# Feed steps, weights by tokens, kept sums and norm weights on GpSimd in a one-layer hybrid decoder step

## The chip, the core and the metric

The kernel runs on one core of one Trainium2 chip. The metric is the time of one execution in device microseconds (us); smaller is better. Before the change three runs gave a median of 1971.52 us (1970.41 to 1973.65).

## The reference, cut to what matters

One layer of a decoder serves a prompt of 1024 tokens and a sample group of 8 sequences with 4 tokens each (1056 tokens in all), with the same weights, in float32:

```
mod = silu(c) @ w_ada + b_ada            -> shift1, scale1, gate1, shift2, scale2, gate2 per sequence
h   = LN(x) * (1 + scale1) + shift1
z   = h @ w_in + b_in                    (1024 -> 6664 columns)
merged = sigmoid(gm) * (mLSTM(z) @ w_branch_m) + sigmoid(ga) * (window_attention(z) @ w_branch_a)
x   = LN(alpha * x + gate1 * (merged @ w_out), ln1_g, ln1_b)
h2  = LN(x) * (1 + scale2) + shift2
u   = h2 @ w_up + b_up                   (1024 -> 5632 columns, a half and b half)
u'  = causal depthwise convolution of width 3 over tokens
f   = (gelu(u'_a) * u'_b) @ w_down + b_down      (2816 -> 1024)
x   = LN(alpha * x + gate2 * f, ln2_g, ln2_b)
```

The outputs are x for both groups, the mLSTM state, the attention caches and the last rows of u for the convolution.

## The kernel before

Activations lie transposed, features on the partitions and the 1056 tokens along the free axis, in 43 equal slots of SBUF ([128, 1056] each). `slot` takes the slot that has been free longest and `drop` returns one; whoever writes a slot anew waits for its last readers. Tokens are cut into three ranges TT of 384, 384 and 288; for the norms into nine row tiles (eight of 128 tokens, and tile 8 with the 32 sample tokens). Each product of two float32 operands is three matmuls of rounded parts (high x high, high x low, low x high); a weight is loaded as `wraw` by SP, rounded on ScalarE to `whi` (L429), and the rest `wlo` is taken on VectorE, in the down projection on GpSimd (L433). `Stream.prep(i)` writes these two, loading first if needed; `load(i)` issues DMAs up to weight i; `ahead_of(i)` preps i+1 and loads i+2. All DMAs spoken of here are issued by SP's queue, in order.

The order of instructions on every engine is the order in which the Python program writes them. TensorE's products are the main line. Work beside it is written as generators in `sides`: after each part of a product, `pulse` adds the part's length to a clock and lets the first generator go on by `rate` steps per us of that clock. What stands between two `yield`s is one step.

From 1060 us on the trace goes through these stages:

- Output projection (w_out) in three token ranges with three PSUM banks L in turn, evacuated by ScalarE (`scaled`, L1695, L1698). After each range a side `out_side` is appended: `residual` (transposes back to rows, VectorE's alpha-sum L1628 and statistics, `norm_factor` on GpSimd, `norm_act` on ScalarE L1604, gain on GpSimd L1635, bias on VectorE L1640, statistics and norm again, rows stored as x1D), then `make_h2` (transposes, ScalarE L1664 and L1669, VectorE L1670). Seven steps of `residual` and seven of `make_h2` per range.
- Up projection: five blocks by token ranges, three direct, sixteen pairs of blocks in a fast scheme (L1507), four direct again (L1752 evacuates on ScalarE). Blocks go to DRAM (uD, yD).
- Feed: a side that reads u back chunk by chunk (22 of 128 features), runs the convolution (`conv`: ScalarE's first tap L1762 with small copies L1763 to L1767, VectorE's two long taps L1769 and L1771, the sample taps L1773, L1774), gelu on ScalarE (L1866), the multiplication by the other half on VectorE (L1876), and the split into high (ScalarE L1884) and low (VectorE L1887). Gelu, multiplication and split belong to the chunk before the one whose taps run.
- Down projection in five groups of 5, 5, 4, 4, 4 chunks. The first three go column block by column block, `down_block` adds to eight tiles facc on VectorE (L1984). The fourth, `down_by_tokens`, goes token range by token range, two column blocks for each of its four weights (k counts 0 to 11), scales by gate2 on ScalarE (L2016), and when a range is done a side `pre` transposes its sums to rows (L198 into PD), adds alpha*x to them (L1945, x fetched from x1D at L1934) and stores the row tile as preD (L1947).
- Last stage: the fifth group, `product` (L2146), has tokens on the partitions: 24 matmuls of 512 columns for each row tile. `fetch` loads preD (L2128); VectorE multiplies by gate2 and adds (L2154, L2155) and takes statistics (L307 to L309); GpSimd makes the factor (L300, L301, L1600); ScalarE normalizes (L1604); the multiplication by ln2_g (L2172) is on GpSimd for the tiles in BY_POOL and on VectorE for the others; the addition of ln2_b (L2173) is on GpSimd; SP stores (L2180). Tile 8 runs on VectorE (L2177, L2178).

Of the kernel before, what the change touches and what calls it, by code (L numbers as in the profile page):

```python
# [11 lines left out]
F32 = mybir.dt.float32  # L12
# [3 lines left out]
OP = mybir.AluOpType  # L16
AX = mybir.AxisListType

D = 1024
# [13 lines left out]

RATE_T, RATE_U, RATE_V, RATE_D, RATE_P = 0.5, 0.5, 0.9, 0.8, 0.8
ROOM = 5
RATES = [0.442, 0.395, 0.35, 0.45, 0.463, 0.495, 1.0, 0.7, 0.417]


STRIPS = [(0, 256), (256, 256), (512, 256), (768, 128), (896, 128)]
# [66 lines left out]
def hybrid_step(ctx: ExitStack, tc: tile.TileContext, I, O):  # L106
# [18 lines left out]
    def slot(dt=F32, name="s"):  # L125
        i = free_slots.popleft()
        count[0] += 1
        t = slots.tile([128, TOK], dt, name=f"{name}_{count[0]}", tag=f"slot{i}", bufs=1)
        tag_of[id(t)] = (i, t, name)
        return t  # L130

    def drop(*ts):
        for t in ts:
            free_slots.append(tag_of.pop(id(t))[0])
# [379 lines left out]
    up_at, dn_at = [], []  # L514
# [852 lines left out]
    hf = {}  # L1367
# [226 lines left out]
    def rows_of(i):  # L1594
        return 128 if i < 8 else 32
# [10 lines left out]
    def residual(ti, r1, tiles, fetch, gb, bb_, done):  # L1606


        ids = [3 * ti + a for a in range(3)]
        st = {}  # L1610
        xs_ = {}
        fetch_at = {0: [0, 1], 1: [2]}
        for s in range(6):
            for a in fetch_at.get(s, ()):
                xs_[a] = fetch(ids[a])
            if s == 0:
                yield
            if s < 3:
                a, n = s, rows_of(ids[s])
                x = xs_[a]  # L1620
                for j in range(8):
                    src, off = r1[j]
                    transpose(pd(j)[:n], src[:, off + a * 128:off + a * 128 + n])
                if a == 2:
                    drop(*tiles)
                for hf in range(2):
                    c = slice(hf * 512, hf * 512 + 512)
                    V.scalar_tensor_tensor(x[:n, c], x[:n, c], ALPHA, PD[hf][:n], op0=OP.mult, op1=OP.add)  # L1628
                mv = ln_stats(x, n)
                st[a] = norm_factor(mv, n)  # L1630
            a = s - 1
            if 0 <= a < 3:
                n = rows_of(ids[a])
                norm_act(xs_[a], st[a], n)
                G.tensor_tensor(xs_[a][:n, :D], xs_[a][:n, :D], gb[:n, :D], op=OP.mult)  # L1635
            a = s - 2
            if 0 <= a < 3:
                n = rows_of(ids[a])
                x = xs_[a]
                V.tensor_tensor(x[:n, :D], x[:n, :D], bb_[:n, :D], op=OP.add)  # L1640
                done(ids[a], n, x)
                mv = ln_stats(x, n)
                st[a] = norm_factor(mv, n)
            a = s - 3
            if 0 <= a < 3:
                norm_act(xs_[a], st[a], rows_of(ids[a]))
            yield
        return [xs_[a] for a in range(3)]

    h2 = mrg  # L1650
# [154 lines left out]

    facc = []
    rows2 = {}
    preD = [dram.tile([128, D], F32, name=f"preD{i}") for i in range(9)]
    acts2 = []

    def kept_rows():
# [23 lines left out]
    def feed():  # L1835

        js, got = [j for c in chunks_of for j in c], {}

        def load(n):
            if n < len(js) and n not in got:  # L1840
                ds = [uD[js[n]], yD[22 + js[n]] if 22 + js[n] in yD else uD[22 + js[n]]]
                got[n] = [slot(name="ld") for _ in ds]
                for t, d in zip(got[n], ds):
                    S.dma_start(t, d)

        load(0)
        load(1)
        yield
        prev = None
        for n in range(len(js) + 1):  # L1850
            cur = None
            if n < len(js):
                while len(free_slots) < ROOM:
                    yield
                load(n + 1)
                j, (u, y2) = js[n], got.pop(n)
                if 22 + j not in yD:
                    u2, y2 = y2, slot(name="y")
                    yield from conv(22 + j, u2, y2)
                    drop(u2)  # L1860
                    yield
                cur = slot(name="y"), y2
                taps = conv(j, u, cur[0])
                next(taps)
            if prev:
                A.activation(prev[0], prev[0], AF.Gelu_apprx_tanh)  # L1866
            yield
            if cur:
                next(taps)
                if len(free_slots) > ROOM:  # L1870
                    load(n + 2)
            yield
            if cur:
                next(taps)
            if prev:
                V.tensor_tensor(prev[0], prev[0], prev[1], op=OP.mult)  # L1876
                drop(prev[1])
            yield
            if cur:
                next(taps, None)  # L1880
                drop(u)
            if prev:
                hi, lo = slot(F32R, "ahi"), slot(F32R, "alo")
                A.copy(hi, prev[0])  # L1884
            yield
            if prev:
                V.tensor_tensor(lo, prev[0], hi.bitcast(F32), op=OP.subtract)  # L1887
                drop(prev[0])
                acts2.append((hi, lo))
            yield  # L1890
            prev = cur
            if n == 10:
                yield from gate_rows2()
        yield from kept_rows()
# [28 lines left out]

    there = set()

    def pre(ti):

        xs_ = {}
        ids = [3 * ti + a for a in range(3)]

        def fetch(i):
            if i in ids:
                xs_[i] = slot(name="x1r")
                S.dma_start(xs_[i][:rows_of(i), :D], x1D[i][:rows_of(i)])  # L1934

        fetch(ids[0])
        for i in ids:
            n, x = rows_of(i), xs_[i]
            fetch(i + 1)
            for j in range(8):  # L1940
                transpose(pd(j)[:n], facc[j][:, i * 128:i * 128 + n])
            yield
            for hf_ in range(2):
                c = slice(hf_ * 512, hf_ * 512 + 512)
                V.scalar_tensor_tensor(x[:n, c], x[:n, c], ALPHA, PD[hf_][:n], op0=OP.mult, op1=OP.add)  # L1945
            yield
            S.dma_start(preD[i][:n], x[:n, :D])  # L1947
            there.add(i)
            drop(xs_.pop(i))
        if ti == 2:  # L1950
            drop(*facc)

# [8 lines left out]
    def operands(gi):  # L1961
        base = sum(KG[:gi])
        n = 0
        while len(acts2) < base + KG[gi]:
            step_side()
            n += 1
            assert n < 200
        return {k: acts2[base + k] for k in range(KG[gi])}
# [30 lines left out]
    def down_by_tokens(gi):  # L1999

        a = operands(gi)
        for ti in range(3):
            t0, nt = TT[ti]
            np_ = nt if ti < 2 else 256
            for q in range(4):
                s_ = dn_at[gi] + q
                k = ti * 4 + q
                if k < 3:
                    win.ahead_of(s_)
                elif k > 6 and k < 11:  # L2010
                    win.prep(dn_at[gi] + k - 3)
                    win.load(dn_at[gi] + k - 2)
                for j in (2 * q, 2 * q + 1):
                    down_block(gi, j, ti, a)
                    f = facc[j][:, t0:t0 + np_]
                    A.activation(f, f, AF.Copy, scale=modT[:, 5, j, 0:1])  # L2016
                    if ti == 2:
                        f = to3(facc[j][:, SEQ:])
                        V.tensor_tensor(f, f, mod_bcast(5, j), op=OP.mult)
                if ti == 2:  # L2020
                    win.done(s_)
            summed.append(ti)
            if not ti:
                spread(pre_rows(), 1.3)
        for k in a:
            drop(*a[k])
# [90 lines left out]
    rate[0] = RATES[6]  # L2117
    gi = len(KG) - 1
    a = operands(gi)
    ln2g, ln2b = bcast_row(I["ln2_g"]), bcast_row(I["ln2_b"])  # L2120
    xs_ = {}

    def fetch(i):
        if i < 9:
            while i not in there:
                pulse(0.4)
            xs_[i] = slot(name="pre")
            S.dma_start(xs_[i][:rows_of(i), :D], preD[i][:rows_of(i)])  # L2128

    for i in range(3):  # L2130
        fetch(i)
    gp, gs = rows2["gp"], rows2["gs"]
    banks = deque([PG, PE_, PF, *L])
    bank_of = {}
    BY_POOL = (0, 2, 4)

    def product(i, hf):
        n, t0 = rows_of(i), i * 128
# [42 lines left out]
        drop(xs_.pop(i))  # L2181

    for i, hf in [(0, 0), (1, 0), (0, 1), (1, 1)] + [(i, hf) for i in range(2, 9) for hf in range(2)]:
        if hf == 0:
            fetch(i + 3)
        product(i, hf)
        add(i, hf)
        if hf:
            stats(i)
            if i:  # L2190
                gains(i - 1)
# [36 lines left out]
```

## Time and profile before

| | |
|---|---|
| median of three runs | 1971.52 us |
| the profiled execution | 1973.88 us, its span 1972.1 us |
| TensorE busy | 1909.6 us of the span, 97% |
| VectorE, ScalarE, GpSimd busy | 1077.3, 803.2, 470.6 us |
| mean granted TensorE clock | 0.991 of full speed |
| moved by DMA | 237.74 MB, 121 GB/s on average |

The span runs from the first to the last instruction. A share of busy time is a mean over stages with different limits; a busy PE is a modelled figure, since matmuls overlap. Idle time of an engine other than the limiting one costs nothing by itself.

### The profile page before, as it was taken

How to read it: one execution, taken by the hardware profiler on the slowest of the kernel's cores; microseconds unless marked ns; L12 is line 12 of the kernel's file. 1: busy time of each engine (PE TensorE's matmuls, PEld its weight loads, DVE VectorE, ACT ScalarE, POOL GpSimd, SP SyncE). 2: the span in 40 equal slices, each digit the busy share in tenths (PEclk: the TensorE clock that was granted, in tenths of full speed). 3: DMA queues.
4: the chain of work that ended last, by engine and by line, in shares of the span. 5: the costliest groups of instructions: out<-in, count | busy, mean ns of one | idle time of the engine just before them, and what ended most of it. 6: DMA issues, size and time to landing. Idle time of an engine off the chain costs nothing. (4 is left out here: it accounts for less than half of the span.)

```text
span 1972.1 us, 33018 instructions
## 1 busy us (share of the span) xinstructions
PE 1909.6 (97%) x12981; PEld 1818.6 (92%) x12981; DVE 1077.3 (55%) x2297; ACT 803.2 (41%) x1796; POOL 470.6 (24%) x591
## 2 busy tenths in 40 slices
PE   6999999999999999999999999999999998999887
PEld 4899999999999989898999999999999998999875
DVE  5454454444644445341454456766666567598658
ACT  4534334343555455331322355333333246654421
POOL 2013233232123031200000333134343310222127
PEclk9999999999999999999999999999999999999989
DMA  9151414334220312398424141432323365344363
GB/s 291 47 140 25 141 30 125 76 79 97 74 77 23 112 54 79 110 342 256 159 83 132 55 128 46 153 109 88 130 88 101 118 225 173 110 139 153 105 227 126
DMA packets 235302, 237.74 MB, mean 121 GB/s; under 512 B 11857, under 2 KB 207105, under 8 KB 235113
## 3 DMA queue, kind: packets, MB, share of 16 engines
q1 hardware_dynamic: 234365, 235.01, 38.9%
q8 instruction: 102, 1.67, 0.4%
q10 hardware_dynamic: 780, 0.61, 0.1%
q14 instruction: 55, 0.45, 0.1%
HBM read 174.93 MB, written 62.68 MB: 120 GB/s over the span
## 5 line engine op out<-in xcount | busy, mean ns | idle before, releaser
L455 PE MATMUL L<-hhi,whi 128*128 128x384 f32 (+1 forms) x1600 | 526.3, 329 | 0.1
L455 PE MATMUL L<-hlo,whi 128*128 128x384 f32 (+1 forms) x1600 | 517.2, 323 | 0.0
L455 PE MATMUL L<-hhi,wlo 128*128 128x384 f32 (+1 forms) x1600 | 516.7, 323 | 0.0
L455 PEld LDWEIGHTS L<-hhi,whi 128*128 128x128 f32 x1600 | 301.7, 189 | 6.6 <-issue 4.8
L455 PEld LDWEIGHTS L<-hlo,whi 128*128 128x128 f32 x1600 | 301.9, 189 | 0.3
L455 PEld LDWEIGHTS L<-hhi,wlo 128*128 128x128 f32 x1600 | 301.6, 188 | 0.0
L433 DVE TENSOR_TENSOR wlo<-wraw,whi 128x1024 fp32r<-128x1024 f32 (+1 forms) x89 | 108.5, 1220 | 114.4 <-ACT whi L429 112.9
L455 PE MATMUL L<-mhi,whi 128*128 128x384 f32 (+1 forms) x480 | 159.4, 332 | 7.8 <-ACT u L1752 3.6
L455 PE MATMUL L<-mhi,wlo 128*128 128x384 f32 (+1 forms) x480 | 156.5, 326 | 0.6 <-DVE wlo L433 0.6
L455 PE MATMUL L<-mlo,whi 128*128 128x384 f32 (+1 forms) x480 | 156.1, 325 | 0.0
L455 PE MATMUL L<-ahi,whi 128*128 128x384 f32 (+1 forms) x432 | 142.3, 329 | 11.0 <-ACT u L1752 3.3
L455 PE MATMUL L<-ahi,wlo 128*128 128x384 f32 (+1 forms) x432 | 140.2, 325 | 3.6 <-POOL wlo L433 3.6
L455 PE MATMUL L<-alo,whi 128*128 128x384 f32 (+1 forms) x432 | 140.1, 324 | 0.0
L429 ACT CAST whi<-wraw 128x1024 fp32r<-128x1024 f32 (+1 forms) x116 | 115.7, 998 | 9.8 <-DMA wraw<-in_w_down 5.1
L433 POOL TENSOR_TENSOR wlo<-wraw,whi 128x640 fp32r<-128x640 f32 (+1 forms) x27 | 55.4, 2053 | 248.8 <-ACT whi L429 149.7
L300 POOL TENSOR_SCALAR rstd<-mv 128x1 f32<-128x1 f32 (+1 forms) x36 | 21.8, 605 | 382.6 <-DVE mv L309 381.3
L455 PEld LDWEIGHTS L<-mhi,whi 128*128 128x128 f32 x480 | 91.4, 190 | 10.1 <-ACT u L1752 4.5
L1481 POOL TENSOR_TENSOR fw<-fraw,fw 128x512 fp32r<-128x512 f32 x32 | 43.2, 1365 | 239.4 <-ACT fw L1477 192.1
L455 PEld LDWEIGHTS L<-ahi,whi 128*128 128x128 f32 x432 | 81.6, 189 | 14.4 <-ACT u L1752 4.2
L455 PEld LDWEIGHTS L<-mhi,wlo 128*128 128x128 f32 x480 | 91.1, 190 | 1.2 <-DVE wlo L433 1.2
L455 PEld LDWEIGHTS L<-mlo,whi 128*128 128x128 f32 x480 | 91.4, 191 | 0.1
L455 PEld LDWEIGHTS L<-ahi,wlo 128*128 128x128 f32 x432 | 81.7, 189 | 4.4 <-POOL wlo L433 4.3
(541 smaller groups left out, 4178.1 us busy)
## 6 DMA issues: line engine op xcount, KB each, us to landing
wraw<-in_w_in SPq DMA_DIRECT2D x52, 512.0 KB
ld<-ff SPq DMA_DIRECT2D x44, 528.0 KB
wada<-in_w_ada SPq DMA_DIRECT2D x44, 512.0 KB
fraw<-in_w_up SPq DMA_DIRECT2D x32, 512.0 KB
ff<-fdst SPq DMA_DIRECT2D x16, 528.0 KB
ff<-y SPq DMA_DIRECT2D x16, 528.0 KB
ff<-u SPq DMA_DIRECT2D x12, 528.0 KB
wraw<-in_w_up SPq DMA_DIRECT2D x12, 512.0 KB
```

Source lines behind the costliest of these rows:

```text
L300: G.tensor_scalar(r[:n], var, eps, None, op0=OP.add)
L429: A.copy(hi[:, :n], t[:, :n])
L433: self.low_by.tensor_tensor(lo[:, :n], t[:, :n], hi[:, :n].bitcast(F32), op=OP.subtract)
L455: T.matmul(ps[:, :nt], x[:, c], y[:, t0:t0 + nt], start=i == 0, stop=i == last)
L1481: (G if p in (1, 4) else V).tensor_tensor(lo, self.src[p], hi.bitcast(F32), op=OP.subtract)
```

## The change

- `residual` has one more `yield` at each of its steps 1 to 4, and RATES[3] and RATES[4] (output projection and first up tiles) go from 0.45 to 0.57 and from 0.463 to 0.6.
- The feed's step order: gelu of the chunk before comes ahead of the new chunk's first tap, the multiplication ahead of the long taps, high and low parts one step earlier; five steps as before.
- `down_by_tokens` preps its second weight ahead of the loop, and at k = 0 and 1 the weight two steps ahead; loads run one weight further.
- `pre` fetches the x rows of the next row tile across the token ranges too; sums of row tiles 3 to 8 stay in their slots (`kept`) instead of going to preD and back.
- In the last stage the three `preD` loads come ahead of the loads of ln2_g and ln2_b, the wait for a row tile's sum stands behind its product, and BY_POOL holds tiles 0 to 6.

```diff
-RATES = [0.442, 0.395, 0.35, 0.45, 0.463, 0.495, 1.0, 0.7, 0.417]
+RATES = [0.442, 0.395, 0.35, 0.57, 0.6, 0.495, 1.0, 0.7, 0.417]
...
                 norm_act(xs_[a], st[a], rows_of(ids[a]))
             yield
+            if 0 < s < 5:
+                yield
...
-    preD = [dram.tile([128, D], F32, name=f"preD{i}") for i in range(9)]
+    preD = [dram.tile([128, D], F32, name=f"preD{i}") for i in range(3)]
...
                 taps = conv(j, u, cur[0])
-                next(taps)
             if prev:
                 A.activation(prev[0], prev[0], AF.Gelu_apprx_tanh)
-            yield
+            if cur:
+                next(taps)
+            yield
+            if prev:
+                V.tensor_tensor(prev[0], prev[0], prev[1], op=OP.mult)
+                drop(prev[1])
             if cur:
                 next(taps)
                 if len(free_slots) > ROOM:
                     load(n + 2)
             yield
-            if cur:
-                next(taps)
-            if prev:
-                V.tensor_tensor(prev[0], prev[0], prev[1], op=OP.mult)
-                drop(prev[1])
-            yield
-            if cur:
-                next(taps, None)
-                drop(u)
             if prev:
                 hi, lo = slot(F32R, "ahi"), slot(F32R, "alo")
                 A.copy(hi, prev[0])
+            if cur:
+                next(taps)
             yield
             if prev:
                 V.tensor_tensor(lo, prev[0], hi.bitcast(F32), op=OP.subtract)
                 drop(prev[0])
                 acts2.append((hi, lo))
+            if cur:
+                next(taps, None)
+                drop(u)
+            yield
             yield
...
+    kept = {}
+    x1s = {}
+
+    def x1_fetch(i):
+        if i < 9 and i not in x1s:
+            x1s[i] = slot(name="x1r")
+            S.dma_start(x1s[i][:rows_of(i), :D], x1D[i][:rows_of(i)])
...
-        fetch(ids[0])
+        x1_fetch(ids[0])
         for i in ids:
-            n, x = rows_of(i), xs_[i]
-            fetch(i + 1)
+            n, x = rows_of(i), x1s[i]
+            x1_fetch(i + 1)
...
-            S.dma_start(preD[i][:n], x[:n, :D])
+            if i < 3:
+                S.dma_start(preD[i][:n], x[:n, :D])
+                drop(x1s[i])
+            else:
+                kept[i] = x
             there.add(i)
-            drop(xs_.pop(i))
...
         a = operands(gi)
+        win.prep(dn_at[gi] + 1)
...
                 if k < 3:
-                    win.ahead_of(s_)
+                    win.prep(s_ + 2 if k < 2 else s_ + 1)
+                    win.load(s_ + 3)
...
-    ln2g, ln2b = bcast_row(I["ln2_g"]), bcast_row(I["ln2_b"])
...
     for i in range(3):
         fetch(i)
+    ln2g, ln2b = bcast_row(I["ln2_g"]), bcast_row(I["ln2_b"])
...
-    BY_POOL = (0, 2, 4)
+    BY_POOL = (0, 1, 2, 3, 4, 5, 6)
...
-        if hf == 0:
-            fetch(i + 3)
         product(i, hf)
+        while i not in there:
+            pulse(0.4)
+        if i > 2:
+            xs_[i] = kept[i]
         add(i, hf)
```

## Rows read from the trace of the kernel before

**Rows 1.** The page's head and its first part: the span, and the busy time of TensorE's matmuls (PE) and weight loads (PEld), VectorE (DVE), ScalarE (ACT) and GpSimd (POOL).

```profile
span 1972.1 us, 33018 instructions
...
PE 1909.6 (97%) x12981; PEld 1818.6 (92%) x12981; DVE 1077.3 (55%) x2297; ACT 803.2 (41%) x1796; POOL 470.6 (24%) x591
```

**Rows 2.** Busy time of each engine by stretch: from and to in us, length, then busy us (and instructions) of PE, PEld, DVE, ACT, POOL, the granted clock of TensorE as a share of full speed, the DMA share and GB/s.

```profile
1100.00:1176.00 76.00, 71.92 (x473) 70.35 (x472) 39.41 (x64) 34.04 (x55) 35.09 (x50) 0.98 0.32 98
...
1207.00:1232.00 25.00, 23.69 (x140) 21.11 (x139) 12.41 (x33) 14.63 (x26) 5.89 (x9) 1.00 0.13 42
1232.00:1597.00 365.00, 365.00 (x2925) 364.73 (x2924) 237.94 (x394) 120.08 (x263) 130.17 (x96) 1.00 0.34 113
1597.00:1680.00 83.00, 74.32 (x459) 72.47 (x459) 60.08 (x74) 51.68 (x109) 3.20 (x2) 0.98 0.65 223
...
1760.00:1824.00 64.00, 62.51 (x389) 62.09 (x388) 53.69 (x70) 30.67 (x60) 16.92 (x7) 1.00 0.45 148
1824.00:1860.00 36.00, 28.54 (x151) 26.47 (x150) 25.22 (x32) 18.43 (x30) 7.38 (x3) 0.95 0.28 89
1860.00:1896.00 36.00, 34.17 (x233) 32.99 (x232) 20.17 (x33) 12.43 (x21) 9.58 (x4) 1.00 0.58 187
1896.00:1916.00 20.00, 12.70 (x53) 10.34 (x53) 6.20 (x12) 1.20 (x3) 0.00 (x0) 0.74 0.79 295
...
1959.00:1972.10 13.10, 0.23 (x1) 0.00 (x0) 9.29 (x10) 1.24 (x1) 7.83 (x6) 0.65 0.24 92
```

**Rows 3.** Who waited for whom, PE alone, the whole span: the waiting line, what it waited for, us in total, times, longest.

```profile
PE PD L198 <- DVE x1r L1945: 9.0, 3, 7.3
PE L L455 <- ACT u L1752: 7.0, 6, 2.7
...
PE L L455 <- POOL wlo L433: 3.6, 2, 1.8
...
PE L L455 <- ACT r L1698: 2.9, 1, 2.9
```

**Rows 4.** Timeline of ScalarE in the output projection: start us, us, instruction, idle time before it and what ended it.

```profile
1158.02 1.25 ACT L1604 ACTIVATE xr<-xr,nbias,rstd 128x1024 f32<-128x1024 f32 x1 [3.49 <-POOL nbias L1600]
1162.73 1.24 ACT L1604 ACTIVATE xr<-xr,nbias,rstd 128x1024 f32<-128x1024 f32 x1 [3.46 <-POOL nbias L1600]
```

**Rows 5.** Timeline of ScalarE where the feed starts, the casts of a chunk's high half.

```profile
1625.07 1.08 ACT L1884 CAST ahi<-y 128x1056 fp32r<-128x1056 f32 x1 [3.66 <-DVE y L1876]
...
1631.60 1.08 ACT L1884 CAST ahi<-y 128x1056 fp32r<-128x1056 f32 x1 [2.12 <-DVE y L1876]
...
1642.31 1.07 ACT L1884 CAST ahi<-y 128x1056 fp32r<-128x1056 f32 x1 [4.98 <-DVE y L1876]
```

**Rows 6.** Timeline of PE at the third weight of the group by tokens.

```profile
1842.79 0.44 PE L455 MATMUL L<-ahi,whi 128*128 128x384 f32 x1 [1.56 <-ACT whi L429]
...
1845.22 0.44 PE L455 MATMUL L<-ahi,wlo 128*128 128x384 f32 x1 [1.81 <-POOL wlo L433]
```

**Rows 7.** Timeline of ScalarE at the same place.

```profile
1841.19 0.61 ACT L2016 ACTIVATE facc<-facc,modT 128x384 f32<-128x384 f32 x1 [2.21 <-DVE facc L1984]
1841.71 1.03 ACT L429 CAST whi<-wraw 128x1024 fp32r<-128x1024 f32 x1
```

**Rows 8.** Timeline of VectorE at the start of the last stage.

```profile
1908.70 1.28 DVE L1945 SCALAR_TENSOR_TENSOR x1r<-x1r,PD 128x512 f32<-128x512 f32 x2 [11.60 <-DMA x1r<-x1D]
```

**Rows 9.** Timeline of PE in the last stage, to 1921 us.

```profile
1909.44 1.97 PE L198 MATMUL PD<-cst,facc 128*128 128x128 f32 x8 [7.30 <-DVE x1r L1945]
...
1912.92 0.63 PE L2146 MATMUL PF<-wlo,ahi 128*128 128x512 f32 x1
1913.35 0.63 PE L2146 MATMUL PF<-whi,alo 128*128 128x512 f32 x1
...
1915.55 0.39 PE L2146 MATMUL PF<-whi,alo 128*128 128x512 f32 x1
1915.78 0.39 PE L2146 MATMUL PF<-whi,ahi 128*128 128x512 f32 x1
...
1920.12 0.40 PE L2146 MATMUL L<-whi,ahi 128*128 128x512 f32 x1
```

**Rows 10.** Timeline of GpSimd in the last stage: the multiplication and addition of the norm weights (L2172, L2173) and the first step of the factor (L300).

```profile
1924.72 2.41 POOL L2172 TENSOR_TENSOR pre<-pre,brow 128x1024 f32<-128x1024 f32 x1
...
1936.09 2.40 POOL L2172 TENSOR_TENSOR pre<-pre,brow 128x1024 f32<-128x1024 f32 x1
1938.57 2.41 POOL L2173 TENSOR_TENSOR pre<-pre,brow 128x1024 f32<-128x1024 f32 x1
1941.07 1.07 POOL L300 TENSOR_SCALAR rstd<-mv 128x1 f32<-128x1 f32 x1
...
1943.11 2.40 POOL L2173 TENSOR_TENSOR pre<-pre,brow 128x1024 f32<-128x1024 f32 x1
```

**Rows 11.** Timeline of VectorE at the end of the last stage: two multiplications by the norm weight, and the last step of the sample tile.

```profile
1951.00 2.44 DVE L2172 TENSOR_TENSOR pre<-pre,brow 128x1024 f32<-128x1024 f32 x1
...
1957.53 1.17 DVE L2172 TENSOR_TENSOR pre<-pre,brow 128x1024 f32<-128x1024 f32 x1
...
1965.56 3.35 DVE L2178 SCALAR_TENSOR_TENSOR pre<-pre,rstd,brow 32x1024 f32<-32x1024 f32 x1 [0.45 <-POOL rstd L301]
```

**Rows 12.** Timeline of SP's queue at the end.

```profile
1968.94 0.33 SPq L2180 DMA_DIRECT2D out_ys<-pre  x1
```

More of the change, by code (lines that the diff above doesn't have):

```diff
@@ L1924, in hybrid_step @@
     there = set()
+    kept = {}
[4 more added lines that the diff above has]
+            S.dma_start(x1s[i][:rows_of(i), :D], x1D[i][:rows_of(i)])
     def pre(ti):
-        xs_ = {}
         ids = [3 * ti + a for a in range(3)]
[L1931 to L1934, printed above, removed]
-        fetch(ids[0])
+        x1_fetch(ids[0])
         for i in ids:
-            n, x = rows_of(i), xs_[i]
-            fetch(i + 1)
+            n, x = rows_of(i), x1s[i]
+            x1_fetch(i + 1)
             for j in range(8):
@@ L2119, in hybrid_step @@
     a = operands(gi)
-    ln2g, ln2b = bcast_row(I["ln2_g"]), bcast_row(I["ln2_b"])
     xs_ = {}
     def fetch(i):
[L2124 to L2128, printed above, removed]
+        xs_[i] = slot(name="pre")
+        S.dma_start(xs_[i][:rows_of(i), :D], preD[i][:rows_of(i)])
     for i in range(3):
         fetch(i)
+    ln2g, ln2b = bcast_row(I["ln2_g"]), bcast_row(I["ln2_b"])
     gp, gs = rows2["gp"], rows2["gs"]
```

## The prediction

> **What bounds the kernel now.** I read the head of the page first: TensorE is busy for 1909.6 of 1972.1 us [rows 1]. A change that takes no matmul away can win only where TensorE stands still or runs at half clock, and in the tail after its last matmul. So the second view is the busy time by stretch [rows 2]: a stretch's length less its PE time is what TensorE lost, and (1 minus the granted clock) times the length is what the half clock (1.2 instead of 2.4 GHz) cost. From 1232 to 1597 us nothing is lost. The rest, in us:
> - 1100 to 1232, output projection and first up tiles: 4.08 + 1.31 idle, and 0.02 x 76 = 1.5 at the lower clock: 6.9.
> - 1597 to 1680, where the feed starts: 8.68, and 0.02 x 83 = 1.7: 10.4.
> - 1760 to 1824: 1.5.
> - 1824 to 1860, start of the group by tokens: 7.46, and 0.05 x 36 = 1.8: 9.3.
> - 1860 to 1916, the residual sums: 1.83 + 7.30, and the clock, below, 2.0: 11.1.
>
> That is 39.2 us. Behind it comes a tail: PE has 0.23 us of work after 1959, so 1972.1 - 1959.2 = 12.9 us belong to the norm and the stores. The third view, who waited for whom on PE, names the causes [rows 3]: the transposes of the sums behind x1r, evacuations on ScalarE that come late, and weights split on GpSimd.
>
> The drops of the clock are no accidents beside these stalls: at 1909.44 TensorE had been idle 7.30 us, and its 512-column matmuls then stand 0.43 us apart (1912.92, 1913.35) where 0.23 (1915.55, 1915.78) is usual [rows 9]. Some ten of them (1911 to 1915) at 0.2 more are the 2.0 us above. In the stretches shown the clock falls below 1.00 only where such stalls lie, and in the tail [rows 2]. I count the rest of the loss as leaving with its stall.
>
> **The change part by part.**
>
> *Norm steps.* In the stage of 1100 to 1232 the loop norm (ScalarE), gain (GpSimd), bias and statistics (VectorE), rstd (GpSimd), norm takes 4.7 us: norms start at 1158.02 and 1162.73, and ScalarE stands 3.46 us for the second [rows 4], with the projection's evacuations queued behind it. A side step is written every 1/0.45 = 2.2 us of TensorE's work, so four steps fall some 2.5 us further behind each. With the extra yields a step is 2/0.57 = 3.5 us: 1.2 behind. Three banks rotate and a group of 384 tokens is about 4.2 us, so a lag up to some 8 us is free. The old lag of 7 to 8 us plus the first norm's wait just passed that, the new one of some 4 doesn't. Steps per tile go from 14 to 18, and 14/0.45 = 31.1 against 18/0.57 = 31.6 us: the tile is done as early as before. What gets denser is the making of h2, whose steps come every 1.7 instead of 2.2 us; ScalarE is its cover, and if that is gone TensorE waits at the transposes. No row shows this density. Bounds: all 6.9 gained, or 2 lost. I take 5.5, near the upper end since the 3.46 us wait is the row next to it.
>
> *Feed.* Each chunk has five steps before and after. Before, ScalarE casts chunk n-1 after the multiplication, which VectorE does behind both long taps of chunk n, which need ScalarE's first tap of n. So ScalarE idles 3.66, 2.12 and 4.98 us ahead of the casts, and casts follow each other by 6.5 and 10.7 us [rows 5], where the steps give 5/0.9 = 5.6 us. Evacuations of the up blocks wait behind. After, gelu goes ahead of the taps, the multiplication ahead of VectorE's taps, and the cast one step earlier. The idle time ahead of the cast goes, but ScalarE now waits at the next gelu for the last taps, so the loop is shorter, not gone; and the same VectorE work stays, 60.08 us busy of 83 [rows 2]. The DMAs are the same and in the same order; prefetch is checked after one more slot is dropped, which can only help it. Bounds: 8 of the 10.4 gained, or 4 lost if VectorE waits for a gelu that is one step away instead of two. I take 4 gained. The 1.5 us at 1760 to 1824 I leave.
>
> *Weights by tokens.* TensorE waits 1.56 us for a high half and 1.81 us for a low half of the same weight [rows 6], and the same pair again 7 us later. The high half was cast at 1841.71, directly behind the gate scaling of a block at 1841.19, which itself waited 2.21 us for VectorE [rows 7]: the cast is queued behind work of the step before. Now this cast is written before the first block, so only the weight's DMA holds it; GpSimd's 2.4 us [rows 10] follow under the two steps of 4.2 us each. Both pairs, some 6 us of the stretch's 7.46, and the 1.8 of the clock could go: 8. Against it: the weight two steps ahead is loaded at that very place, so ScalarE stands until it lands, and the feed's last chunks, with the block additions behind them on VectorE, stand too. I take 4.5, between -1 and 8. On the slots: walking through the allocations by hand, the tightest place goes from two free slots to one, so loads wait for slots just released; each of these is released by work TensorE has already passed, and I cost it at nothing, up to 2 in the range.
>
> *x a tile ahead, six tiles kept.* VectorE waited 11.60 us for x1r of tile 6 [rows 8], because that load was written at the start of a tile and came behind gain rows and early sums on SP, itself held by the stores of sums. Now it is written during tile 5, and the stores of tiles 3 to 8 and their six loads (5.25 MB) are gone. The 7.30 us and the 2.0 of the clock go. Tile 7 is still loaded behind three sums and two gain rows; it is needed about 9 us into the last stage, so 0 to 4 us can come back. The 1.83 us at 1860 to 1896 stays: it is VectorE's order, not a load. I take 9, between 5 and 11.
>
> *Norm weights on GpSimd, last stage.* Here the change costs. A tile that GpSimd multiplies and adds takes it, with the next rstd, from 1936.09 to 1943.11: 7.02 us [rows 10]. TensorE needs 24 x 0.232 = 5.6 us a tile. Before, only tiles 0, 2 and 4 did this, so GpSimd kept up. Now seven tiles in a row do. The first multiplication began 4.6 us after the fourth product, whose successor starts at 1920.12 (to 1924.72) [rows 9, 10]; with S as the stage's start, the fourth product ends at S + 4 x 2.79 + two transpose sets of 1.0 = S + 13.1, the chain starts at S + 17.7, and seven rounds end at S + 66.8 with the factor of tile 8. The sample tile's last step then takes 3.35 us beside GpSimd's last addition [rows 11] and its store, issued at 1968.94, ended the span 3.2 later [rows 12]: S + 73.4. TensorE ends at S + 18 x 2.79 + 3.0 = S + 53.2. So the tail is 20 us instead of 12.9: 7 lost. VectorE's relief (five multiplications of 1.17 to 2.44 us [rows 11]) is off the path. Bounds: 9 lost, or 1 gained.
>
> The Trainium skill (SBUF — State Buffer, Who interferes with whom) has it that a VectorE instruction with two SBUF inputs contends with a GpSimd one that reads SBUF, and the second to issue is blocked until the first is done. The trace agrees: the multiplication on VectorE took 2.44 us beside GpSimd's addition and 1.17 alone [rows 11]. Judged by that rule alone, taking these five off VectorE ends a collision and the stage would get shorter; that is the first rival.
>
> **Sum:** 5.5 + 4 + 4.5 + 9 - 7 = 16 us. The profiled execution took 1973.88 us with its span of 1972.1; 16 less is 1957.9. It lay 2.4 above the median 1971.52, so for a median: 1955.5, say 1955.
>
> **Rivals.**
> - *The tail isn't paid.* GpSimd's chain is shorter than 7.02, or VectorE's relief counts: the last stage ends 12 us behind TensorE, and the gain is 23 to 24: 1948. For it: VectorE loses up to 1.3 us to each collision [rows 11]. Against: the 7.02 is measured with nothing else on GpSimd.
> - *Only loads and weights count.* Feed and norm steps give nothing, since the VectorE work stays: 4.5 + 9 - 7 = 6.5: 1965.
> - *Slower: the one-step multiplication.* VectorE meets the multiplication one step (1/0.8 = 1.25 us) behind gelu instead of two. If ScalarE lags by a step, VectorE stands there with the block additions behind it, about 1.1 us for each of 22 chunks, 24 us. Once more than 16 of them reach TensorE the rest is a loss; all of them make 1971.5 + 8 = 1980. For it: VectorE is 53.69 of 64 us busy from 1760 to 1824 [rows 2]. Against: the three banks hide a lag of some two blocks.
> - *The weights aren't ahead:* the cast waits for its DMA as long as it did for the queue. 4.5 less: 1960, inside the forecast's range.
>
> **How the numbers follow.** Forecast 0.58, tail not paid 0.18, only loads and weights 0.15, slower 0.07, weights not ahead 0.02. The forecast's own range is 1949 to 1962; the neighbours stretch it to 1944 to 1966. A measurement here can't tell less than 0.2% (3.9 us) from no change. All cases but the slower one lie below 1967.6, with a little at their edge: faster 0.90, same 0.04, slower 0.06.
>
> **What would show it.** Right: PE idle at 1896 to 1916 gone and no 0.43 us spacing there; no PE wait for a low half on GpSimd in the group by tokens; GpSimd without a gap from its first gain to the end, 7 us a tile, and some 20 us between the last matmul and the end. Wrong: a tail of 13 us; new waits of VectorE at L1866's result; PE waiting for transposes of h2.

## The result, and the profile after

The changed kernel takes 1960.49 us (median of 4 runs, 1958.75 to 1961.27) against 1971.49 for the kernel before: a ratio of 0.9942, interval 0.9924 to 0.9959, or 11.0 us less. Forecast were 1955 and 16 less. The time lies inside the forecast's own range, but the parts don't add up the way I had them. The profiled execution took 1961.27 us with its span of 1959.5, 12.6 less than the span before.

The page's head, and below it the busy time by stretch, both of the changed kernel, with the columns of [rows 1] and [rows 2]:

```profile
span 1959.5 us, 32996 instructions
...
PE 1904.9 (97%) x12981; PEld 1815.8 (93%) x12981; DVE 1075.2 (55%) x2293; ACT 804.9 (41%) x1796; POOL 478.5 (24%) x595
...
1100.00:1176.00 76.00, 73.18 (x481) 72.42 (x481) 38.98 (x64) 34.40 (x55) 34.45 (x50) 0.98 0.30 98
...
1597.00:1680.00 83.00, 77.40 (x480) 75.99 (x479) 60.69 (x71) 52.99 (x108) 5.92 (x3) 0.98 0.68 229
1760.00:1824.00 64.00, 60.27 (x371) 59.08 (x369) 55.28 (x68) 29.55 (x58) 16.60 (x7) 1.00 0.46 154
1824.00:1860.00 36.00, 32.50 (x194) 31.75 (x195) 25.80 (x38) 19.49 (x34) 7.22 (x3) 1.00 0.36 119
...
1896.00:1916.00 20.00, 20.00 (x94) 16.24 (x93) 16.05 (x28) 3.73 (x3) 9.31 (x12) 1.00 0.17 65
```

The stretch from 1896 to 1916, with 7.30 us idle before, is now full at full clock. The group by tokens (1824 to 1860) has 3.5 us idle instead of 7.46. But 1760 to 1824 lost 1.5 before and loses 3.7 now, and the first stretch, where [rows 4] showed the norm loop, still loses 2.8 of 4.1. Who PE waited for, from 1597 us on, the first two answers from 1597 to 1700 and 1700 to 1824, the third from 1824 to 1860:

```profile
PE L L455 <- ACT u L1754: 2.6, 2, 2.0
PE L L455 <- DVE fdst L1530: 1.7, 1, 1.7
...
PE L L455 <- DVE facc L1992: 3.3, 3, 2.0
...
PE L L455 <- DVE facc L1992: 4.0, 3, 2.0
```

The waits for u (ScalarE's late evacuations, 7.0 us in [rows 3]) are down to 2.6 us, and those for low halves on GpSimd from 3.6 to 0.4. In their place stands VectorE's block addition (L1992).

Both kernels run the same 12981 matmuls in the same order, so the stages can be measured between the same matmuls: the time from the start of one to the start of another, whatever the stages before did. This ledger is worked out in that way from the profiled execution of each kernel; the columns are named after the numbers of the matmuls, "to 6901" is the start of the 6901st, and "tail" is the span less the end of the last matmul (1959.23 before, 1942.24 after). From the start of the 12901st to that end it is 18.8 or 18.9 us in every kernel, and has no column.

| kernel | to 6901 | 6901–8101 projection, norm | 8101–11101 | 11101–11701 feed starts | 11701–12301 feed | 12301–12601 by tokens | 12601–12901 sums, last stage | tail | median us |
|---|---|---|---|---|---|---|---|---|---|
| before | 1034.5 | 198.6 | 376.0 | 107.2 | 98.3 | 59.9 | 65.9 | 12.9 | 1971.49 |
| changed | 1035.2 | 197.7 | 377.0 | 102.7 | 100.8 | 53.8 | 56.0 | 17.3 | 1960.49 |
| before + feed alone | 1033.0 | 198.8 | 376.0 | 101.1 | 101.1 | 56.8 | 65.7 | 12.9 | 1965.93 |
| before + GpSimd's seven tiles | 1034.0 | 198.7 | 376.0 | 107.2 | 98.2 | 58.4 | 64.7 | 16.4 | 1973.94 |
| changed, old norm steps | 1034.6 | 198.7 | 376.0 | 101.1 | 100.9 | 54.8 | 55.7 | 17.5 | 1959.56 |
| changed, gain on VectorE | 1036.6 | 194.7 | 377.1 | 102.5 | 102.5 | 54.0 | 55.7 | 17.3 | 1957.83 |
| changed, old feed | 1034.0 | 197.2 | 377.0 | 107.2 | 98.8 | 58.4 | 55.9 | 17.2 | 1966.40 |
| changed, old weights | 1035.3 | 197.4 | 377.0 | 102.6 | 100.8 | 53.8 | 56.1 | 17.5 | 1960.91 |
| changed, x at the start | 1036.5 | 197.3 | 377.0 | 102.6 | 100.9 | 53.9 | 60.1 | 16.9 | 1965.75 |
| changed, all sums by DRAM | 1033.9 | 197.5 | 377.0 | 102.6 | 100.8 | 54.4 | 58.6 | 17.3 | 1963.84 |
| changed, GpSimd three tiles | 1035.3 | 198.1 | 377.0 | 102.5 | 100.9 | 54.1 | 56.1 | 13.6 | 1956.69 |
| candidate 1 | 1032.7 | 198.4 | 376.0 | 101.2 | 99.1 | 56.0 | 55.8 | 14.2 | 1954.32 |
| candidate 2 | 1034.0 | 197.0 | 376.0 | 101.1 | 99.1 | 57.7 | 55.7 | 12.2 | 1952.74 |
| candidate 3 | 1034.5 | 196.7 | 376.0 | 102.1 | 99.1 | 56.3 | 55.8 | 12.2 | 1953.58 |

The first column is code that none of these kernels touches, and it spreads from 1032.7 to 1036.6: so much of a median's difference can be chance. Part of this goes with the clock: cut into stretches of 50 us, the time from 500 to 850 us has one stretch with a granted clock of 0.97 instead of 1.00 in candidate 1, and three with the gain on VectorE. Most other columns repeat within 0.3 us where the code is the same, but not all: with the new norm steps the projection's goes from 197.2 to 198.1, and the feed's and the group by tokens can differ by 1.5 us and more, with the clock or, from 59.9 to 58.4, without a cause that I know. Each row is one execution.

From before to changed the columns give -0.7 + 0.9 - 1.0 + 4.5 - 2.5 + 6.1 + 9.9 - 4.4 = 12.8 us (12.6 by the spans).

### The profile page after: what moved, and what is told of

The parts are those of the page before. It is cut to its first block, busy times and chain, and to the rows that moved or that the text cites. A ratio compares the mean times of both kernels' runs of the same rounds, so it can differ in the third digit from the quotient of the medians.

```text
span 1959.5 us, 32996 instructions
## 1 busy us (share of the span) xinstructions
PE 1904.9 (97%) x12981; PEld 1815.8 (93%) x12981; DVE 1075.2 (55%) x2293; ACT 804.9 (41%) x1796; POOL 478.5 (24%) x595
## 2 busy tenths in 40 slices
DMA packets 233766, 232.24 MB, mean 119 GB/s; under 512 B 11665, under 2 KB 206913, under 8 KB 233577
## 5 line engine op out<-in xcount | busy, mean ns | idle before, releaser
L433 POOL TENSOR_TENSOR wlo<-wraw,whi 128x640 fp32r<-128x640 f32 (+1 forms) x27 | 57.7, 2138 | 239.9 <-ACT whi L429 183.3
L300 POOL TENSOR_SCALAR rstd<-mv 128x1 f32<-128x1 f32 (+1 forms) x36 | 18.2, 506 | 372.2 <-DVE mv L309 371.0
```

The source lines that it names most:

```text
L300: G.tensor_scalar(r[:n], var, eps, None, op0=OP.add)
L433: self.low_by.tensor_tensor(lo[:, :n], t[:, :n], hi[:, :n].bitcast(F32), op=OP.subtract)
```

## The experiments

**GpSimd's seven tiles.** In the changed kernel:

```diff
-    BY_POOL = (0, 1, 2, 3, 4, 5, 6)
+    BY_POOL = (0, 2, 4)
```

> The changed kernel with the norm weights back as they were: GpSimd multiplies tiles 0, 2 and 4 only. Theory (the tail is GpSimd's chain of seven tiles, 6.2 us each against TensorE's 5.6): GpSimd keeps up, the tail behind the last matmul goes from 17.3 back to about 13 us, and the kernel takes 4 to 5 us less than the changed one, about 1956. Rival (VectorE's relief pays for it): VectorE's multiplications beside GpSimd take 2.3 us instead of 1.2, the tail stays at 17, and the time stays at 1960.

Measured 1956.69 us (ratio to before 0.992, 0.9904 to 0.9937), tail 13.6: the theory. The reverse edit on the kernel before:

> The kernel before with this one part of the change alone: GpSimd multiplies tiles 0 to 6. Theory: TensorE ends where it did, the tail grows from 12.9 to about 17.3 us, 1976. Rival: no longer tail, 1971.5, since in the kernel before the last stage begins with 7 us of idle time that the chain can use.

Measured 1973.94 (1.001, 1.0001 to 1.002). The tail grew to 16.4 as the theory has it; the time by 2.4 only: this profile shows 1.5 less in the group by tokens, where nothing was edited, and 1.2 less in the last stage. The second goes with the clock, 0.83 from 1896 to 1916 here and 0.74 before [rows 2]; the first I can't tie to anything. GpSimd in the changed kernel, its first multiplication and the end of its chain, with VectorE's first step of the sample tile in its place:

```profile
1908.43 2.41 POOL L2179 TENSOR_TENSOR pre<-pre,brow 128x1024 f32<-128x1024 f32 x1
...
1938.09 0.22 POOL L300 TENSOR_SCALAR rstd<-mv 128x1 f32<-128x1 f32 x1
...
1944.20 0.22 POOL L300 TENSOR_SCALAR rstd<-mv 128x1 f32<-128x1 f32 x1
...
1947.82 3.20 POOL L2180 TENSOR_TENSOR x1r<-x1r,brow 128x1024 f32<-128x1024 f32 x1
1948.75 3.35 DVE L2184 SCALAR_TENSOR_TENSOR x1r<-x1r,mv,brow 32x1024 f32<-32x1024 f32 x1
1951.11 1.07 POOL L300 TENSOR_SCALAR rstd<-mv 32x1 f32<-32x1 f32 x1
```

A round is 6.1 us (1944.20 - 1938.09), not the 7.02 of [rows 10]: the factor's first step takes 0.22 instead of 1.07, because no multiplication by the norm weights runs on VectorE beside it. At 1951.11, beside the sample tile's (L2184), it takes 1.07 again.

**Norm steps.** Undone, and then instead with the gain moved:

```diff
-RATES = [0.442, 0.395, 0.35, 0.57, 0.6, ...
+RATES = [0.442, 0.395, 0.35, 0.45, 0.463, ...
...
-            if 0 < s < 5:
-                yield
```

> The changed kernel with the old norm steps (no further yields, old rates). Theory by the stage's account (1100 to 1232 us lost 6.9 before and 5.5 after): 1 to 1.5 us more, all of it in that stage: 1961.5. Rival: the extra yields moved the wait to the first weights of the up projection without any gain, and the time is the same or up to 1 us less.

Measured 1959.56 (0.994, 0.9926 to 0.9955). The stage itself costs 1.0 more, as the theory has it, and with the gain on GpSimd all kernels agree: 198.4 to 198.8 with the old steps, 197.2 to 198.1 with the new ones. But the ledger's next columns give 1.0 and 1.6 back. In the first lies the 1.7 us wait for fdst, above (at 1607), which is not there without the extra steps; the second is not explained. So the steps are worth nothing, or less.

```diff
-                G.tensor_tensor(xs_[a][:n, :D], xs_[a][:n, :D], gb[:n, :D], op=OP.mult)
+                V.tensor_tensor(xs_[a][:n, :D], xs_[a][:n, :D], gb[:n, :D], op=OP.mult)
```

> The changed kernel with one edit in the norm steps of the output projection: the multiplication by the gain goes from GpSimd to VectorE. Theory (GpSimd is the loop: multiplication 2.4 and two factors of 1.1 and 2.1 us give 4.9 a step, whatever the density of the steps): ScalarE's waits for the second norm's factor, 3.47 and 3.24 us, fall under 2, the stage from 1100 to 1232 loses 2 to 3 instead of 5.5 us, 1957.5. Rival (VectorE's own queue or the weights' casts behind the norms set it): the waits stay over 3 us and the time stays at 1960.

Measured 1957.83 (0.9933, 0.9919 to 0.9948; it overlaps with the changed kernel's), the stage 3.0 us shorter: from 1100 to 1232 us TensorE is idle for 1.3 us less, and the clock, 0.98 from 1100 to 1176 in the changed kernel, is 1.00. GpSimd's multiplications by the gain and the first step of the factor between them, ScalarE's norms and the cast behind them, and PE, all in the changed kernel:

```profile
1157.62 2.40 POOL L1635 TENSOR_TENSOR xr<-xr,brow 128x1024 f32<-128x1024 f32 x1
1160.11 1.25 POOL L300 TENSOR_SCALAR rstd<-mv 128x1 f32<-128x1 f32 x1
...
1162.54 2.41 POOL L1635 TENSOR_TENSOR xr<-xr,brow 128x1024 f32<-128x1024 f32 x1
...
1162.41 1.24 ACT L1604 ACTIVATE xr<-xr,nbias,rstd 128x1024 f32<-128x1024 f32 x1 [3.47 <-POOL nbias L1600]
...
1167.33 1.24 ACT L1604 ACTIVATE xr<-xr,nbias,rstd 128x1024 f32<-128x1024 f32 x1 [3.24 <-POOL nbias L1600]
...
1168.90 1.05 ACT L429 CAST whi<-wraw 128x1024 fp32r<-128x1024 f32 x1
...
1170.00 0.44 PE L455 MATMUL L<-mhi,whi 128*128 128x384 f32 x1 [2.17 <-ACT whi L429]
```

and the same norms and the same matmul with the gain on VectorE:

```profile
1159.79 1.25 ACT L1604 ACTIVATE xr<-xr,nbias,rstd 128x1024 f32<-128x1024 f32 x1 [2.86 <-POOL nbias L1600]
...
1163.51 1.24 ACT L1604 ACTIVATE xr<-xr,nbias,rstd 128x1024 f32<-128x1024 f32 x1 [2.48 <-POOL nbias L1600]
...
1169.94 0.44 PE L455 MATMUL L<-mhi,whi 128*128 128x384 f32 x1 [0.92 <-ACT whi L429]
```

GpSimd goes without a gap from one multiplication by way of a factor and a small scaling to the next in 4.9 us (1157.62 to 1162.54), and so the norms follow each other by 4.9; without the multiplication they follow by 3.7. The waits didn't fall under 2, but the loop's engine is named. With the wider steps PE no longer waits for evacuations (2.9 us for r in [rows 3]) but for the first weight's cast, which stands behind the same norms.

**Feed.** The old order in the changed kernel, and the new one alone in the kernel before (the diff of the change, by itself):

> The changed kernel with the old feed order. Theory by the matmuls' starts in both traces (the new order wins 3.5 us by 1715 and loses 2.5 of it again from 1771 to 1795): about 1 us more, 1961.5, with no wait of TensorE for a block addition at 1774. Rival: the loss from 1771 on is not the feed's but comes with the kept tiles or the weights; then the old feed costs the whole 3.5 us, 1964, and that wait stays.

> The kernel before with the new feed order alone. Theory (undone in the changed kernel it cost 5.9 us, and the weights two steps ahead gave nothing): 5 to 6 us less than before, 1966, with the gain around 1650 and in the group by tokens. Rival (the feed's gain needs the weights ahead or the new norm steps): 0 to 3 us less, 1969 to 1971.

Measured 1966.40 (0.9975, 0.9965 to 0.9985) and 1965.93 (0.9969, 0.9956 to 0.9982): undone it costs 5.9 us, alone it brings 5.5. I had expected 1 for the first. The loss of 2 to 3 us at 11701–12301 is the feed's, for the old order gives it back; what I had missed is the group by tokens, 58.4 with the old feed and 53.8 with the new one, part of it by the clock (0.95 and 1.00 from 1824 to 1860). First who waited for whom on ScalarE and VectorE, from 1597 to 1870 us before and then from 1597 to 1860 in the changed kernel:

```profile
ACT ahi L1884 <- DVE y L1876: 70.6, 20, 6.2
DVE y L1876 <- ACT y L1866: 1.2, 1, 1.2
...
ACT ahi L1881 <- DVE y L1872: 17.6, 8, 3.5
ACT y L1867 <- DVE y L1776: 41.6, 16, 4.2
DVE y L1872 <- ACT y L1867: 14.8, 11, 3.4
```

ScalarE waits 17.6 us ahead of the casts instead of 70.6, and 41.6 at the next gelu for the last taps; VectorE now waits 14.8 us at the multiplication for gelu (L1867, before L1866). Then the new wait of TensorE, with VectorE and GpSimd, in the changed kernel:

```profile
1768.69 2.26 DVE L1886 TENSOR_TENSOR alo<-y,ahi 128x1056 fp32r<-128x1056 f32 x1
1770.87 0.24 DVE L1775 SCALAR_TENSOR_TENSOR y<-us,vT,y 128x32 f32<-128x32 f32 x1
1771.15 2.35 DVE L1776 SCALAR_TENSOR_TENSOR y<-us,vT,y 128x32 f32<-128x32 f32 x1
1773.43 1.37 DVE L1992 TENSOR_TENSOR facc<-L,facc 128x384 f32<-128x384 f32 x3
...
1771.09 4.84 POOL L433 TENSOR_TENSOR wlo<-wraw,whi 128x1024 fp32r<-128x1024 f32 x2 [1.25 <-DVE alo L1886]
...
1774.12 0.41 PE L455 MATMUL L<-ahi,whi 128*128 128x384 f32 x1 [1.96 <-DVE facc L1992]
```

The low half and the last taps are one step in the new order. Three additions stand behind them, from 1768.69 to 1773.43, and the last tap of 32 columns takes 2.35 us instead of 0.25 while GpSimd makes a weight's low half. Last the group by tokens with the old feed, ScalarE, VectorE, PE:

```profile
1838.29 1.05 ACT L429 CAST whi<-wraw 128x1024 fp32r<-128x1024 f32 x1 [4.62 <-DMA wraw<-in_w_down]
1839.25 1.24 ACT L1764 ACTIVATE y<-ld,vT 128x1024 f32<-128x1024 f32 x1
...
1840.52 2.42 DVE L1771 SCALAR_TENSOR_TENSOR y<-ld,vT,y 128x1023 f32<-128x1023 f32 x1 [5.36 <-ACT y L1764]
...
1846.04 0.62 PE L455 MATMUL L<-ahi,whi 128*128 128x384 f32 x1 [5.20 <-DVE facc L1991]
```

The cast waits for its weight, the first tap waits behind the cast, VectorE's taps for that, the additions behind these, and TensorE at the end of the line. In the new order the gelu stands in the tap's place.

**Weights by tokens.**

```diff
-        win.prep(dn_at[gi] + 1)
...
-                    win.prep(s_ + 2 if k < 2 else s_ + 1)
-                    win.load(s_ + 3)
+                    win.ahead_of(s_)
```

> The changed kernel with the old loads and casts of the weights in the group by tokens. In the run with the old feed the 6 us which TensorE won in this group were lost again although the weights were still prepared two steps ahead. Theory A (it takes both): the low halves on GpSimd are late again, 5 to 6 us more in this group, 1966. Theory B (the feed alone wins them, because its last chunks no longer hold up the queues of ScalarE and VectorE there): 0 to 1 us more, 1961, no wait of TensorE for a low half.

Measured 1960.91 (0.9943, 0.9927 to 0.996), 53.8 us in the group with and without. Theory B for the time, though not for its sign: PE waits 2.2 us for low halves again, while its wait for block additions, from 1597 us on, is 5.2 us instead of 7.2. The changed kernel, ScalarE, VectorE and PE:

```profile
1833.90 1.05 ACT L429 CAST whi<-wraw 128x1024 fp32r<-128x1024 f32 x1 [3.86 <-PE L L455]
1834.86 1.08 ACT L1867 ACTIVATE y<-y 128x1056 f32<-128x1056 f32 x1
...
1835.97 2.58 DVE L1872 TENSOR_TENSOR y<-y,ld 128x1056 f32<-128x1056 f32 x1 [1.60 <-ACT y L1867]
...
1841.68 0.42 PE L455 MATMUL L<-ahi,whi 128*128 128x384 f32 x1 [1.58 <-DVE facc L1992]
```

The cast two steps ahead holds ScalarE for 3.86 us, and the feed's gelu and VectorE's multiplication stand behind it: one wait given for another.

The run with the feed alone has the old weights and the new feed too, and yet takes 56.8 us in this group. What TensorE waits for there from 1810 to 1868 us, and the stretch from 1824 to 1860; below it the run with the old weights in the changed kernel, from 1813 to 1868 and the same stretch:

```profile
PE L L455 <- POOL wlo L433: 1.8, 1, 1.8
PE L L455 <- DVE facc L1985: 1.1, 1, 1.1
PE L L455 <- ACT whi L429: 0.9, 1, 0.9
1824.00:1860.00 36.00, 32.17 (x175) 30.88 (x175) 23.59 (x31) 17.36 (x32) 7.17 (x3) 0.91 0.29 91
...
PE L L455 <- DVE facc L1992: 2.0, 1, 2.0
PE L L455 <- POOL wlo L433: 1.8, 1, 1.8
1824.00:1860.00 36.00, 32.95 (x196) 32.19 (x197) 24.57 (x38) 19.71 (x35) 7.20 (x3) 1.00 0.33 108
```

Both wait 3.8 us; the 3.0 us between them go with the clock, 0.91 against 1.00, which is 3.2 us of the 36. Why it fell in the one and not in the other stays open.

**x and the sums.** First x at the start of the tile group, then all nine sums through DRAM (with the old function that fetches them):

```diff
-            x1_fetch(i + 1)
+            if i < ids[2]:
+                x1_fetch(i + 1)
```

> The changed kernel, six sums still kept on chip, but each third tile's x loaded at the start of its tile group, not a tile ahead. Theory (the load's late issue made the 7.3 us idle time): TensorE waits 5 to 8 us for x1r of tile 6 again, 1966 to 1968. Rival (it was the queue of stores of sums and their loads in front): with those gone the load lands in time, and the time stays at 1960 to 1961.

```diff
-            if i < 3:
-                S.dma_start(preD[i][:n], x[:n, :D])
-                drop(x1s[i])
-            else:
-                kept[i] = x
+            S.dma_start(preD[i][:n], x[:n, :D])
+            drop(x1s[i])
```

> The changed kernel with x loaded a tile ahead, but all nine sums stored to DRAM and loaded again, as before. Theory: no idle time at the start of the last stage, at most 2 us more than the changed kernel, 1960 to 1962. Rival: the queue of these transfers holds x or the sums up, 5 us or more, 1965 and above.

Measured 1965.75 (0.996, 0.9946 to 0.9975) and 1963.84 (0.9958, 0.9943 to 0.9973). The five runs of the first go from 1959.89 to 1966.45. In the ledger's column of the last stage the first edit costs 4.1 us and the second 2.6, of the 9.9 that both together win; up to 1.8 of the 4.1 can be the clock, 0.91 from 1896 to 1916 against 1.00. Neither expectation holds in full. VectorE in the changed kernel, and with x at the start:

```profile
1899.16 1.28 DVE L1950 SCALAR_TENSOR_TENSOR x1r<-x1r,PD 128x512 f32<-128x512 f32 x2 [0.75 <-DMA x1r<-x1D]
```

```profile
1897.80 1.28 DVE L1951 SCALAR_TENSOR_TENSOR x1r<-x1r,PD 128x512 f32<-128x512 f32 x2 [6.75 <-DMA x1r<-x1D]
```

Before it was 11.60 us [rows 8]: without the stores and loads of six sums 4.9 us of this wait go, with the early issue 6.0 more. The late load, issued at 1890.60, still stands behind three sums and two gain rows in SP's queue.

**Candidates.** The first is three tiles on GpSimd, old norm steps, and in the feed

```diff
+            yield
             if cur:
                 next(taps, None)
                 drop(u)
-            yield
             yield
```

> A candidate: the changed kernel with GpSimd multiplying tiles 0, 2 and 4, the old norm steps, and in the feed the last taps one step behind the low half, in the step that was empty. Theory: 3.8 us from GpSimd, 0.9 from the norm steps, and of the 3.3 us which TensorE waits for block additions from 1771 to 1795 two, because low half and last taps, 4.9 us of VectorE's queue in one step, are parted: 1954. Rival for the feed part: the next multiplication then comes later and its cast too, no gain there, 1956.

Measured 1954.32 (0.9911, 0.9896 to 0.9926). In the feed the split won 1.8 us (100.9 to 99.1 against the run with old norm steps) and lost 1.2 of it in the group by tokens, where the clock was 0.95 from 1824 to 1860 against 1.00 in that run. The second has besides the old weights, the gain on VectorE, and

```diff
-            G.tensor_tensor(x, x, ln2b[:n, :D], op=OP.add)
+            (V if i == 7 else G).tensor_tensor(x, x, ln2b[:n, :D], op=OP.add)
```

> A second candidate: the first one, with the old weights in the group by tokens, the gain of the output projection's norm on VectorE, and tile 7's last addition on VectorE. Theory: of the 3.1 us wait of TensorE in the group by tokens behind a cast that waits 4.06 us for its weight, 2 go; of the norm steps 2.5; of the tail 2, since the sample tile's last step no longer stands 3.35 us beside GpSimd's addition: 1948. Rival for the tail: VectorE's queue gets longer by 1.2 us, which eats it; for the weights: the low halves are late again (3 us); then 1951 to 1953.

Measured 1952.74 (0.9904, 0.9888 to 0.9921), 4.7 us over the expectation. The tail gave its 2 us (14.2 to 12.2), the norm loop 1.4; the old weights cost 1.7 where I had 2 to win. The last step of the sample tile in the changed kernel and its store, then both in this candidate:

```profile
1952.85 3.35 DVE L2185 SCALAR_TENSOR_TENSOR x1r<-x1r,rstd,brow 32x1024 f32<-32x1024 f32 x1 [0.75 <-POOL rstd L301]
...
1956.23 0.33 SPq L2187 DMA_DIRECT2D out_ys<-x1r  x1
```

```profile
1947.24 1.27 DVE L2181 SCALAR_TENSOR_TENSOR x1r<-x1r,rstd,brow 32x1024 f32<-32x1024 f32 x1
...
1948.54 0.33 SPq L2183 DMA_DIRECT2D out_ys<-x1r  x1
```

With tile 7's addition off GpSimd the step takes 1.27 instead of 3.35 us [rows 11].

> The second candidate with the changed kernel's weights two steps ahead in the group by tokens put back; nothing else differs. Theory by the matmuls' starts of the two candidates (that group lost 2.2 us against the changed kernel with the weights ahead, 3.9 with the old ones): 1 to 2 us less than the second candidate, 1951 to 1952, so the weights ahead are worth a little once the feed is reordered. Rival: nothing, as in the run that undid them in the changed kernel: 1952.7.

Measured 1953.58 (0.9907, 0.989 to 0.9923): no difference to the second. The group by tokens is 1.4 us shorter, as expected; the start of the feed, untouched, 1.0 longer, with a granted clock of 0.98 there where the second had 1.00. The clock need not be the cause: the run with three tiles had 1.00 there too, and the changed kernel 0.98, at 102.5 and 102.7 us. So it stays open whether the weights ahead are worth 1.4 us in this version. All three candidates beat the two kernels of the study.

## Why the prediction was right, and where it wasn't

- *Total.* 16 forecast, 12.6 by the profiled executions, 11.0 by the medians. The mechanism of the largest term and of the loss was right. That the time lies so near is in part luck: the norm steps' miss of nearly 5 us and the tail's of nearly 3 the other way partly cancel.
- *Norm steps, 5.5: wrong.* The step that failed is "a lag up to some 8 us is free": the only queue that I priced behind the late norms was that of the evacuations. The lag did fall, and the 2.9 us wait for r is gone. But the cast of the first up weight stands behind the same norms, and TensorE waits 2.17 us for it, since the density of steps doesn't change the loop: GpSimd's round of a 2.4 us multiplication and a factor keeps the norms 4.9 us apart. 0.9 was won in the stage, and 1.0 to 2.6 lost behind it by the run with the old steps.
- *Feed 4 and weights 4.5.* Together 8.5 against 4.5 - 2.5 + 6.1 = 8.1, but not so divided. The feed alone gave 5.5 and, undone, cost 5.9; the weights gave 0, so that the sum fits by chance. My 0.02 for "the weights aren't ahead" was far too low: the cost against it ("ScalarE stands until it lands, and the feed's last chunks, with the block additions behind them on VectorE, stand too") was written down and priced too low. That this rival's 1960 is next to the measured time is chance. Of the 6.1, the feed alone brings 59.9 to 56.8; the way on to 53.8 goes with the clock, 0.91 against 1.00.
- *Slower rival.* Its place was right, the block additions behind VectorE's feed work, and its price 2 to 3 us instead of 24. VectorE's waits for gelu, a sign of being wrong, did come, 14.8 us of them; at most 7.2 us, all of TensorE's waits for block additions, can have reached TensorE, such as the 1.58 us behind the wait for gelu at 1835.97. In the feed column most of the loss (1.8 of 2.5 us, by the split of candidate 1) came from the low half and last taps in one step.
- *x ahead, 9: right,* 9.9, with the half clock gone as said. Both parts of the edit carry it. The transfers that went are 5.50 MB (237.74 to 232.24 MB), not 5.25.
- *Tail, -7: right in kind, too large.* 4.4 measured, with GpSimd busy without a gap as forecast. The chain began at S + 19.0 (1908.43, with S = 1889.46) instead of S + 17.7, but its seven rounds, the factor of tile 8 included, took 44.4 us to 1952.85 and not 49.1; the last step and store, 6.6 us from there to the end, are as worked out. I took the duration of the factor from rows in which VectorE multiplied beside it, and the change takes just that away. Nor were five multiplications taken off VectorE: it had five, and tile 7's stayed, so four.

The Trainium skill (SBUF — State Buffer, Who interferes with whom), weighed in the prediction, has a VectorE instruction with two SBUF inputs and a GpSimd one that reads SBUF exclude each other. The trace agrees on both sides: the 32-column tap at 2.35 us is VectorE's share, and the 0.22 against 1.07 of L300 is GpSimd's. But by that rule alone the move should have paid; the run with three tiles shows that it cost 3.8 us, because GpSimd's own chain was the longer one.

## What to carry to other kernels

A duration read from a trace includes what ran beside it: when a change takes the neighbour away, take the row where it stood alone. Before steps are made denser or a weight is fetched further ahead, find the engine whose round sets the loop and what is queued behind the new wait; a wait that only moves ahead in an in-order queue holds everything behind it. Measure stages between the same instructions of both kernels: a gain of 5 us and a loss of 4 in one total are two findings.

## What the hardware showed unexpectedly

A GpSimd operation on a single column took 0.22 us alone and 1.07 beside a VectorE multiplication: contention is paid by the smallest operations too. And the same idle time doesn't always bring the half clock. With the gain on VectorE, the stretch from 1760 to 1824 us had 3.96 us idle and a granted clock of 0.97; the changed kernel had 3.73 there and 1.00. The ledger's feed column differs by 1.7 us (102.5 to 100.8) with the same code, and such steps can be part of the spread of the medians.
